# Products of attention weights and values in plain float32, two key blocks at a time in the halves of TensorE's columns

## The chip, the cores and the metric

The program runs on one core of one Trainium2 chip. The metric is the device time of one execution in microseconds (us); lower is better. The engines that matter are PE (TensorE, matmuls and transposes; PEld is its weight load), DVE (VectorE), ACT (ScalarE), POOL (GpSimd) and SP (SyncE, which issues DMAs).

## The reference, cut to what matters

One inference step of a two-layer encoder on 1024 prompt tokens and 8 x 16 sample tokens, width 1024, all in float32. The first layer's mixer runs 8 stick-breaking attention heads beside a convolution module; the second layer's mixer is banded softmax attention with 16 heads. Each layer ends in a squared-ReLU MLP. What the change touches is the last line of the first mixer's attention, the product of weights `w` and values `v` for the prompt tokens:

```python
def stick_breaking(q, k, v, q_pos, k_pos):
    z = jnp.einsum('bqhd,bkhd->bhqk', q, k).astype(jnp.float32) * (HEAD_DIM ** -0.5)
    mask = k_pos[None, :] < q_pos[:, None]
    log_keep = jnp.where(mask, jax.nn.log_sigmoid(-z), 0.0)
    between = lax.cumsum(log_keep, axis=3, reverse=True) - log_keep
    w = jnp.where(mask, jnp.exp(jax.nn.log_sigmoid(z) + between), 0.0)
    return jnp.einsum('bhqk,bkhd->bqhd', w.astype(v.dtype), v)
```

Heads have 64 channels. The mask is causal, so a block of 128 queries meets only the key blocks up to its own.

## The kernel before

**Split products.** Nearly all matmuls take operands in a rounded float32 type (`F32R`). To keep float32 accuracy, an operand is split into a high part (ACT copies it, rounding: L185) and a low part (DVE subtracts the high part from the source: L186), and high x high, high x low and low x high are summed. The helper `split` does both. A few products are in plain `F32` and need no split: the sample tokens' scores `zs` (L507, stationary operands 32 columns wide, four of them in the four quarters of the array's columns), the samples' products `so` (L541, likewise), the sums `mu` (L962), and the transposes.

**The first mixer** (`mixer0`) works through four pairs of heads, p = 0 to 3. Per pair there are 8 jobs (head i = 0, 1; query pair t = 0 to 3, that is 256 queries). A job computes scores `z` on PE (L865 to L868), sigmoids on ACT (L869, L870), a scan over `kp` (L848) and a product into `sg` (L850) on DVE, and then its weighing steps (`weigh_steps`): key blocks of 128 are gathered into groups of up to 512 columns, which here means two blocks a group; `turn` transposes a group's weights on PE into a PSUM bank `tpa` (L394) and splits it into `wha` (ACT) and `wla` (DVE); `prod` multiplies with the values. A job of query pair t has t + 1 groups, the last of which has 256 + 128 columns and the others 256 + 256, so there are 80 groups in all: 48 of 512 columns and 32 of 384. The stationary operand `vs` holds 128 columns per key block, the 64 high and the 64 low parts of the values, so one matmul gives the high sum in PSUM partitions 0 to 63 and the low one in 64 to 127; a group has four matmuls (`wha` and `wla` for each of two blocks, L406). `finish` copies the lower sum out (`ata`, L414, ACT) and adds the two halves (`cpa`, L416, DVE).

**Beside it** in the same stretch run the input projections of the next pair (`psp`, `psg`, `psa`, L225, PE, with their weights split into `hl_wi`), the sample tokens' attention, and the convolution: 124 taps, each one DVE instruction over 128 x 1024 and one over 128 x 128 (`y`, L674). `merge` interleaves the lists of steps by their declared PE time, with lags after a named step; `level` spreads the taps in proportion to the DVE time that the steps declare. The tile framework then schedules each engine's queue. Taps are traced inside `tc.issue_after(prior["weights"].ins)`: in DVE's queue a tap stands behind the instruction that `prior["weights"]` last named, which is the newest `wla`.

The second mixer uses the same `weigh_steps`.

Of the kernel before, what the change touches and what calls it, by code (L numbers as in the profile page):

```python
# [8 lines left out]
F32 = mybir.dt.float32  # L9
F32R = mybir.dt.float32r  # L10
AF = mybir.ActivationFunctionType
ALU = mybir.AluOpType
# [3 lines left out]
P = 128  # L16
# [7 lines left out]
HD = 64  # L24
# [13 lines left out]
PASS = 1 / 2.4  # L38


def f(ap):
    return ap.bitcast(F32)
# [56 lines left out]
def run(steps):  # L99
    for s in steps:  # L100
        s.go()
# [23 lines left out]
def tile_trunk(ctx, tc, ins, outs):  # L125
    nc = tc.nc
    ACT = nc.scalar.activation
    tt = nc.vector.tensor_tensor
    stt = nc.vector.scalar_tensor_tensor
    mm = nc.tensor.matmul  # L130
# [3 lines left out]
    def pool(name):  # L134
        return tc.tile_pool(name=name, bufs=1, reuse_waits="tile")
# [7 lines left out]
    def bank(name):  # L143
        return psum.tile([P, 512], F32, tag="ps", name=name)


    ident = const.tile([P, P], F32, name="ident")
# [35 lines left out]
    def split(hi, lo, src):  # L183

        ACT(hi, src, AF.Copy)  # L185
        return tt(lo, src, f(hi), ALU.subtract)  # L186

    prior = {}
# [184 lines left out]
    def weigh_steps(vs, wk, cat, i, t, blocks, name, scored):  # L373


        order = sorted(blocks.keys, key=lambda j: -len(blocks.keys[j]))
        groups, cur, used = [], [], 0
        for j in order:
            n = P * len(blocks.keys[j])
            if used + n > 512:  # L380
                groups.append((cur, used))
                cur, used = [], 0
            cur.append((j, used, n))
            used += n
        groups.append((cur, used))
        nmm = 2 * len(order)
        st = {"done": 0, "w": {}}

        def turn(gi):
            items, used = groups[gi]  # L390
            tp = bank(f"tp{name}{gi}")
            for j, c0, n in items:
                for q, tile_q in enumerate(blocks.keys[j]):
                    nc.tensor.transpose(tp[:, c0 + q * P:c0 + (q + 1) * P], blocks.get(j, tile_q), ident)  # L394
            wh = wk.tile([P, 512], F32R, tag="wt", name=f"wh{name}{gi}")
            wl = wk.tile([P, 512], F32R, tag="wt", name=f"wl{name}{gi}")
            prior["weights"] = split(wh[:, :used], wl[:, :used], tp[:, :used])
            st["w"][gi] = (wh, wl)

        def prod(gi):  # L400
            if gi == 0:
                st["av"] = bank(f"av{name}")
            for src in st["w"][gi]:
                for j, c0, n in groups[gi][0]:
                    o0 = 0 if 2 * t in blocks.keys[j] else P
                    mm(st["av"][:, o0:o0 + n], vs[:, j, i].rearrange("p a d -> p (a d)"), src[:, c0:c0 + n],  # L406
                       start=st["done"] == 0, stop=st["done"] == nmm - 1)
                    st["done"] += 1

        def finish():  # L410
            own = slice(64 * i, 64 * i + 64)
            av = st["av"]
            tmp = wk.tile([P, 256], F32, tag="av", name=f"at{name}")
            ACT(tmp[own], av[64:128, :256], AF.Copy)  # L414
            piece = wk.tile([P, 256], F32, tag="cat", name=f"cp{name}")
            tt(piece[own], av[0:64, :256], tmp[own], ALU.add)  # L416
            cat.put(piece, own, t * 256, 256)

        def pcost(gi):
            return sum(2 * max(n, 256) * PASS for _, _, n in groups[gi][0])  # L420

        def tcost(gi):
            return groups[gi][1] / P * 109

        last = len(groups) - 1
        def dcost(gi):
            return 60 + groups[gi][1] / 0.96

        def turns(gi):
            return Step(tcost(gi), lambda: turn(gi), dcost(gi), f"turn{name}{gi}", None if gi else scored, 4500)  # L430

        lag = 4500 if cat.layer == 0 else 2500

        def prods(gi):
            if gi < last:
                return Step(pcost(gi), lambda: prod(gi), 0.0, None, f"turn{name}{gi}", lag)
            return Step(pcost(gi), lambda: (prod(gi), finish()), 330.0, f"out{name}", f"turn{name}{gi}", lag)

        steps = [turns(0)]
        for gi in range(1, last + 1):  # L440
            steps += [turns(gi), prods(gi - 1)]
        steps.append(prods(last))
        return steps
# [150 lines left out]
    def mixer0():  # L594
        with ExitStack() as st:

            ep = Bufs(st.enter_context(pool("early0")), sg=3, kp=2)
            cp = Bufs(st.enter_context(pool("cache0")), ct=3)
# [5 lines left out]
            pp = Bufs(st.enter_context(pool("pair0")))  # L604
            wk = Bufs(st.enter_context(pool("work0")), wt=4, wts=1, cat=2)
# [3 lines left out]
            order = []  # L609
# [9 lines left out]
            at = {n: i for i, n in enumerate(order)}  # L619
            accs = []  # L620
            n0 = Next(0, rp, Lent(wk, "wt", 512), "h0", accs)
            h, rstd = n0.h, n0.r
# [209 lines left out]
            def expand_v(p, g):  # L832
                v = S["sv", p]
                tp = bank(f"vt0{p}{g}")
                for i in range(3):
                    c = (3 * g + i) * P
                    nc.tensor.transpose(tp[:, i * P:(i + 1) * P], v[:, c:c + P], ident)
                n = 3 if g < 2 else 2
                tv = tp[:, :n * P].rearrange("p (j h d) -> p j h d", j=n, h=2)
                dst = vs[:, 3 * g:3 * g + n]  # L840
                split(dst[:, :, :, 0, :], dst[:, :, :, 1, :], tv)
                if g == 2:
                    S["vn"] = pp.tile([P, P], F32, "vn", f"vn0{p}")
                    ACT(S["vn"], tp[:, 2 * P:3 * P], AF.Copy)
# [55 lines left out]

            start()
            qs, kd, kl = ([ep.tile([P, TP], F32R, f"{n}{i}", f"{n}{i}") for i in range(2)] for n in "qkl")
            vs = pp.tile([P, 8, 2, 2, HD], F32R, "vs", "vs0")
            run(level(proj(0), taps[:TAPS[0]]))
            taps = taps[TAPS[0]:]
            carry, cat_t = [], None
            for p in range(4):
                S["p"] = p
                expand_qk(p)
                if p < 3:  # L910
# [3 lines left out]
                    n = TAPS[p + 1]  # L914
# [8 lines left out]
                cat = Cat(0, p, wk, cat_t)  # L923
                jobs = attend(p, cat)
                body, left = pipeline(jobs[1:], jobs[0][2])
                steps = carry + [jobs[0][0]] + [Step(327.0, lambda p=p, g=g: expand_v(p, g)) for g in range(NG)]
# [111 lines left out]
    def mixer1(nx, win):  # L1038
        h, rstd = nx.h, nx.r
        with ExitStack() as st:  # L1040
            ep = Bufs(st.enter_context(pool("early1")), s=4, bp=2)
            cp = Bufs(st.enter_context(pool("cache1")), ct=2)
            pp = Bufs(st.enter_context(pool("pair1")))
            wk = Bufs(st.enter_context(pool("work1")), ss=1, wt=4, wts=2, cat=3, tot=4, mx0=4, mx1=4)
# [3 lines left out]
            vs = pp.tile([P, 8, 2, 2, HD], F32R, "vs", "vs1")  # L1048
# [79 lines left out]
            def attend(p, cat):  # L1128
                def job(i, t):
                    ws = {}  # L1130

                    def one(q):
                        n = min(q + 1, 5) * P
                        k0 = (q + 1) * P - n
                        b0 = 640 - n
                        s = ep.tile([P, 640], F32, "s", f"s{p}{i}{q}")
                        pieces = []
                        qc = slice(q * P, q * P + P)
                        for c, m in ((0, n),) if n <= 512 else ((0, 384), (384, 256)):
                            z = bank(f"zc{p}{i}{q}{c}")  # L1140
                            kc = slice(k0 + c, k0 + c + m)
                            mm(z[:, :m], qs[i][:, qc], kd[i][:, kc], start=True, stop=False)  # L1142
                            mm(z[:, :m], qs[i][:, qc], kl[i][:, kc], start=False, stop=True)  # L1143
                            pieces.append((z[:, :m], S["bp", p, i][:, b0 + c:b0 + c + m], c, m))
                        softmax(s, pieces, n, f"c{p}{i}{q}")
                        ws[q] = (s, k0)

                    q0, q1 = 2 * t, 2 * t + 1
                    keys = {j: [q for q in (q0, q1) if max(0, q - 4) <= j <= q] for j in range(max(0, q0 - 4), q1 + 1)}
                    blocks = Blocks(keys, lambda j, q: ws[q][0][:, j * P - ws[q][1]:j * P - ws[q][1] + P])  # L1150

                    def cost(q):
                        return 2 * max(256, min(q + 1, 5) * P) * PASS

                    name = f"c{p}{i}{t}"
                    return (Step(cost(q0), lambda: one(q0), 1100.0), Step(cost(q1), lambda: one(q1), 1100.0, f"z{name}"),
                            weigh_steps(vs, wk, cat, i, t, blocks, name, f"z{name}"))

                return [job(i, t) for i in range(2) for t in range(4)]

# [9 lines left out]
            for p in range(8):  # L1170
# [3 lines left out]
                cat = Cat(1, p, wk, cat_t)  # L1174
# [4 lines left out]
                steps = carry + [jobs[0][0]]  # L1179
                steps += [Step(327.0, lambda p=p, g=g: expand_v(p, g)) for g in range(NG)]  # L1180
                if p == 7:
# [3 lines left out]
                    steps = []  # L1185
# [524 lines left out]
    cat = mixer0()  # L1710
# [41 lines left out]
    cat = mixer1(n1, win)  # L1752
# [134 lines left out]
```

## Time and profile before

| | |
|---|---|
| median of 3 runs (lowest to highest) | 2791.39 us (2788.73 to 2793.07) |
| profiled execution | 2792.6 us |
| its span | 2790.7 us |
| PE, DVE, ACT, POOL busy | 96%, 77%, 50%, 12% |
| TensorE's mean granted clock | 0.988 of full speed |

The profiled execution's own time is its span and 1.9 us around it. Busy shares are means over the whole span; the first mixer lies in the first fifth of it, from about 99 us (the first pair's attention) to 586 us.

### The profile page before, as it was taken

The page shows a single profiled execution, that of the slowest core. Times are in us where ns is not written, and L with a number is a line of the kernel's source. Part 1 is how long each engine was busy: PE and PEld are TensorE (multiplying, and loading weights), DVE is VectorE, ACT ScalarE, POOL GpSimd, SP SyncE. Part 2 cuts the span into 40 slices and gives each one's busy share as a digit, 9 for nine tenths or more (in the row PEclk, how much of TensorE's full clock was granted, in tenths as well). Part 3 has the DMA queues.
Part 4 walks back from the last instruction along what each step waited for, and adds up shares of the span by engine and source line. Part 5 has one row for each costly group of instructions (what it writes and reads, how often), then busy time and mean ns, then how long its engine had stood idle before and what let it go on. Part 6 is the DMA issues. An engine that isn't in the chain of part 4 may idle for free.

```text
span 2790.7 us, 50667 instructions
## 1 busy us (share of the span) xinstructions
PE 2688.6 (96%) x19362; PEld 2582.7 (93%) x19362; DVE 2138.3 (77%) x4209; ACT 1389.7 (50%) x2898; POOL 329.3 (12%) x599
## 2 busy tenths in 40 slices
PE   8998988999999999999999999998999999999998
PEld 8987876789999999999999999997999999999998
DVE  8999999988777765758666777778787777647577
ACT  5344445755554453435355555555555555534344
POOL 1000101022111110000011111110231111100001
PEclk9999998999999999999999999999999999999999
DMA  4434346443343467534544444446543333684344
GB/s 155 128 96 127 121 128 194 155 166 131 139 144 144 147 236 250 152 94 146 160 142 137 138 138 138 138 133 211 186 137 139 139 139 135 223 273 137 96 125 142
DMA packets 173203, 422.90 MB, mean 152 GB/s; under 512 B 25968, under 2 KB 53808, under 8 KB 170912
## 3 DMA queue, kind: packets, MB, share of 16 engines
q1 hardware_dynamic: 135696, 288.38, 33.0%
q0 software_dynamic: 37120, 131.27, 13.7%
q8 instruction: 152, 2.49, 0.4%
q14 instruction: 91, 0.75, 0.1%
q10 hardware_dynamic: 144, 0.02, 0.0%
HBM read 289.60 MB, written 117.34 MB: 146 GB/s over the span
## 4 chain that ended last, share of the span: by engine, by line
PE 74%; DVE 17%; ACT 4%; issue 3%; DMA 2%; POOL 0%; DVEq 0%; SPq 0%; ACTq 0%; POOLq 0%
PE pd L1631 25%; PE um L1402 25%; PE psc L225 10%; DVE y L674 4%; DVE kp L848 3%; PE avc L406 2%; PE tpc L394 2%; PE psoa L225 1%; DVE sg L850 1%; PE f L225 1%; PE psob L225 1%; PE zc L1142 1%; DVE wla L186 1%; PE zc L1143 1%; PE psp L225 1%
## 5 line engine op out<-in xcount | busy, mean ns | idle before, releaser
L225 PE MATMUL psc<-h,hl_wc 128*128 128x384 f32 x1728 | 327.1, 339 | 0.0
L225 PEld LDWEIGHTS psc<-h,hl_wc 128*128 128x128 f32 x1728 | 296.8, 188 | 13.3 <-issue 10.9
L1402 PE MATMUL um<-sl,hl_m 128*128 128x288 f32 x1548 | 241.8, 297 | 0.0
L1402 PEld LDWEIGHTS um<-sl,hl_m 128*128 128x128 f32 x1548 | 219.0, 190 | 0.0
L1631 PE MATMUL pd<-tm,hl_wd 128*128 128x288 f32 x1584 | 214.7, 294 | 0.0
L1631 PEld LDWEIGHTS pd<-tm,hl_wd 128*128 128x128 f32 x1584 | 211.3, 189 | 0.0
L674 DVE SCALAR_TENSOR_TENSOR y<-u,dw,y 128x1024 f32<-128x1024 f32 (+1 forms) x232 | 176.4, 807 | 0.4
L225 PE MATMUL psp<-h,hl_wi 128*128 128x384 f32 x864 | 168.5, 344 | 0.2 <-ACT kps L897 0.2
L1409 ACT ACTIVATE hdm<-hdm 128x288 f32<-128x288 f32 x192 | 84.7, 442 | 156.5 <-DVE hdm L1408 154.8
L225 PEld LDWEIGHTS psp<-h,hl_wi 128*128 128x128 f32 x864 | 149.4, 190 | 6.4 <-issue 4.9
L186 DVE TENSOR_TENSOR tm<-xr,tm 128x576 fp32r<-128x576 f32 (+1 forms) x120 | 85.6, 714 | 90.7 <-ACT tm L185 87.0
L185 ACT ACTIVATE tm<-xr 128x576 fp32r<-128x576 f32 (+1 forms) x120 | 77.5, 646 | 92.1 <-PE pd L1631 74.0
L1402 PE MATMUL um<-sl,hl 128*128 128x288 f32 x756 | 119.1, 296 | 0.0
L1109 ACT ACTIVATE s<-s,mxc 128x640 f32<-128x640 f32 (+4 forms) x128 | 88.8, 694 | 59.6 <-DVE mxc L1106 57.9
L1631 PE MATMUL pd<-th,hl_wd 128*128 128x288 f32 x792 | 112.7, 295 | 3.4 <-DVE th L186 3.2
L1631 PE MATMUL pd<-xr,hl_wd 128*128 128x288 f32 x792 | 111.7, 294 | 0.0
L1631 PEld LDWEIGHTS pd<-th,hl_wd 128*128 128x128 f32 x792 | 107.3, 188 | 4.3 <-DVE th L186 3.7
L1631 PEld LDWEIGHTS pd<-xr,hl_wd 128*128 128x128 f32 x792 | 107.2, 189 | 0.0
L1402 PEld LDWEIGHTS um<-sl,hl 128*128 128x128 f32 x756 | 106.4, 188 | 0.8
L1631 PE MATMUL pd<-tm,hl 128*128 128x288 f32 x768 | 104.9, 295 | 0.0
L1631 PEld LDWEIGHTS pd<-tm,hl 128*128 128x128 f32 x768 | 103.1, 188 | 0.0
L1106 DVE CUSTOM_DVE_ANT_0 s<-zc,bp 128x384 f32<-128x384 f32 (+3 forms) x128 | 66.0, 516 | 39.1 <-PE zc L1143 37.1
(527 smaller groups left out, 6774.3 us busy)
## 6 DMA issues: line engine op xcount, KB each, us to landing
xr<-hb_d SPq DMA_DIRECT2D x208, 288.0 KB, 3.0
xr<-in_w_up_dram SPq DMA_DIRECT2D x64, 512.0 KB, 4.2
hb_d<-hdm POOLq DMA_DIRECT2D x96, 288.0 KB, 2.4
hb_d<-t POOLq DMA_DIRECT2D x96, 288.0 KB, 2.4
wm<-in_w_down_dram SPq DMA_DIRECT2D x64, 256.0 KB, 4.2
st_wd<-in_w_down_dram SPq DMA_DIRECT2D x64, 256.0 KB, 3.7
st_wc<-in_w_in_c_dram SPq DMA_DIRECT2D x44, 256.0 KB, 2.9
xm_d<-xo POOLq DMA_DIRECT2D x16, 576.0 KB, 3.6
```

The source lines that it names most:

```text
L185: ACT(hi, src, AF.Copy)
L186: return tt(lo, src, f(hi), ALU.subtract)
L225: mm(ps()[:, :G], hl[:, a, at:at + P], act[g][k // 4][b][:, k % 4, :], start=n == 0, stop=n == len(todo) - 1)
L394: nc.tensor.transpose(tp[:, c0 + q * P:c0 + (q + 1) * P], blocks.get(j, tile_q), ident)
L406: mm(st["av"][:, o0:o0 + n], vs[:, j, i].rearrange("p a d -> p (a d)"), src[:, c0:c0 + n], start=st["done"] == 0, stop=st["done"] == nmm - 1)
L674: stt(src if j == CW - 1 else dst, src, wj, dst, ALU.mult, ALU.add)
L848: nc.vector.tensor_tensor_scan(keep[:, 0:n][:, ::-1], keep[:, 0:n][:, ::-1], ones[:, 0:1].to_broadcast([P, n]), 1.0, ALU.mult, ALU.mult)
L1106: nc.vector.tensor_tensor_reduce(s[:, c:c + m], z, b, -1.0, mx, ALU.add, ALU.min, new)
L1109: ACT(s[:, :n], s[:, :n], AF.Exp, bias=mx, scale=-1.0, accum_out=tot)
L1402: mm(banks[b, n][:, :TQ], w[:, a, c * P:c * P + P], combo(key, c)[:, h, n * TQ:n * TQ + TQ], start=k < 3 and c == 0 and i == 0, stop=c == ...
L1409: ACT(y, y, AF.Relu)
L1631: mm(ps, w[:, a, m * P:m * P + P], b[:, h, (n - ns[0]) * TQ:(n - ns[0]) * TQ + TQ], start=first and s == 0, stop=j == NJ - 1 and s == 2, s ...
```

## The change

The first mixer gets a new `weigh_steps`; the second keeps the old one under the name `split_weigh_steps`. In the new one a group's transposed weights are copied once, in plain float32, by ACT (`wa`, no `wla`); the values are kept in plain float32 (`vs` is half as large, one ACT copy and no subtraction); and a group of two key blocks is two matmuls with 64 stationary columns each, the first block's into PSUM partitions 0 to 63 and the second's into 64 to 127. `finish` adds the two halves as before, and for t = 0, where the second block reaches only 128 of the 256 queries, copies the other 128 from the first half alone. The groups have the same blocks and the declared PE times come out the same; the turns no longer declare DVE time; the tag `wt` with its 4 buffers now holds one tile a group, not two; and `prior["weights"]` now names the newest `cpa`, once a job.

```diff
         order = sorted(blocks.keys, key=lambda j: -len(blocks.keys[j]))
+        groups = []
+        for two in zip(order[::2], order[1::2]):
+            n, m = (P * len(blocks.keys[j]) for j in two)
+            groups.append(([(two[0], 0, n), (two[1], n, m)], n + m))
+        st = {"w": {}}
+
+        def turn(gi):
+            items, used = groups[gi]
+            tp = bank(f"tp{name}{gi}")
+            for j, c0, n in items:
+                for q, tile_q in enumerate(blocks.keys[j]):
+                    nc.tensor.transpose(tp[:, c0 + q * P:c0 + (q + 1) * P], blocks.get(j, tile_q), ident)
+            st["w"][gi] = wk.tile([P, 512], F32, tag="wt", name=f"w{name}{gi}")
+            ACT(st["w"][gi][:, :used], tp[:, :used], AF.Copy)
+
+        def prod(gi):
+
+            if gi == 0:
+                st["av"] = bank(f"av{name}")
+            for m, (j, c0, n) in enumerate(groups[gi][0]):
+                o0 = 0 if 2 * t in blocks.keys[j] else P
+                mm(st["av"][64 * m:64 * m + 64, o0:o0 + n], vs[:, j, i], st["w"][gi][:, c0:c0 + n], start=gi == 0,
+                   stop=gi == last)
+
+        def finish():
+            own = slice(64 * i, 64 * i + 64)
+            av = st["av"]
+            one = P if t == 0 else 0
+            tmp = wk.tile([P, 256], F32, tag="av", name=f"at{name}")
+            ACT(tmp[own, one:], av[64:128, one:256], AF.Copy)
+            piece = wk.tile([P, 256], F32, tag="cat", name=f"cp{name}")
+            if one:
+                ACT(piece[own, :one], av[0:64, :one], AF.Copy)
+            prior["weights"] = tt(piece[own, one:], av[0:64, one:256], tmp[own, one:], ALU.add)
+            cat.put(piece, own, t * 256, 256)
+
+        def pcost(gi):
+            return 4 * groups[gi][0][0][2] * PASS
...
+        def turns(gi):
+            return Step(tcost(gi), lambda: turn(gi), 0.0, f"turn{name}{gi}", None if gi else scored, 4500)
...
+    def split_weigh_steps(vs, wk, cat, i, t, blocks, name, scored):
...
-            prior["weights"] = split(wh[:, :used], wl[:, :used], tp[:, :used])
+            split(wh[:, :used], wl[:, :used], tp[:, :used])
...
-                tv = tp[:, :n * P].rearrange("p (j h d) -> p j h d", j=n, h=2)
-                dst = vs[:, 3 * g:3 * g + n]
-                split(dst[:, :, :, 0, :], dst[:, :, :, 1, :], tv)
+                ACT(vs[:, 3 * g:3 * g + n], tp[:, :n * P].rearrange("p (j h d) -> p j h d", j=n, h=2), AF.Copy)
...
-            vs = pp.tile([P, 8, 2, 2, HD], F32R, "vs", "vs0")
+            vs = pp.tile([P, 8, 2, HD], F32, "vs", "vs0")
...
-                            weigh_steps(vs, wk, cat, i, t, blocks, name, f"z{name}"))
+                            split_weigh_steps(vs, wk, cat, i, t, blocks, name, f"z{name}"))
```

The order of PE's queue is nearly kept. This is PE near the end of pair 0 (last job but one group; `psp` is the next pair's projection, `tpa` the transposes, `ava` the products), before:

```order
L225 MATMUL psp_2241<-h_30_171,hl_wi_0_1816 128x384
L394 MATMUL tpa_2254<-ident,sg_1957 128x128
L394 MATMUL tpa_2254<-ident,sg_2017 128x128 x2
L406 MATMUL ava_2218<-wha_2163,vs_747 128x256 x2
L406 MATMUL ava_2218<-wla_2164,vs_747 128x256 x2
L225 MATMUL psp_2241<-h_40_178,hl_wi_1_1821 128x384
L225 MATMUL psp_2241<-h_41_179,hl_wi_1_1821 128x384
```

and of the change:

```order
L225 MATMUL psp_2182<-h_30_171,hl_wi_0_1776 128x384
L388 MATMUL tpa_2195<-ident,sg_1912 128x128
L388 MATMUL tpa_2195<-ident,sg_1970 128x128 x2
L398 MATMUL ava_2161<-wa_2108,vs_747 64x256 x2
L225 MATMUL psp_2182<-h_40_178,hl_wi_1_1781 128x384
L225 MATMUL psp_2182<-h_41_179,hl_wi_1_1781 128x384
```

The group stands at the same place, behind the next group's transposes and between two halves of a projection's matmuls; its four matmuls of 128 rows are two of 64 (64x256 is the shape written).

This is DVE at the end of pair 0 (the last scan `kp` and its `sg`, the job's closing add `cpa`, and `l`, `q`, which belong to the next pair's expansion), before:

```order
L848 SCALAR_TENSOR_TENSOR kp_2226<-kp_2226,ones 128x1024
L816 TENSOR_TENSOR sv_2156<-psp_2167,rh_315 128x384
L850 TENSOR_TENSOR sg_2225<-sg_2225,kp_2226 128x1023
L186 TENSOR_TENSOR wla_2259<-tpa_2254,wha_2258 128x384
L674 SCALAR_TENSOR_TENSOR u_389<-u_389,dw,y_1236 128x1024
L674 SCALAR_TENSOR_TENSOR u_389<-u_389,dw,y_1236 128x8x16
L577 COPY cs_1918<-sq_2282 64x64 x2
L416 TENSOR_TENSOR cpa_2295<-ava_2218,ata_2293 64x256
L351 TENSOR_TENSOR l_745<-sk_1914,k_743 64x1024
L351 TENSOR_TENSOR l_746<-sk_1914,k_744 64x1024
L353 SCALAR_TENSOR_TENSOR q_742<-sq_1181,q_742 64x1024
```

and of the change:

```order
L879 TENSOR_TENSOR sv_2101<-psp_2110,rh_315 128x384
L737 SCALAR_TENSOR_TENSOR u_389<-u_389,dw,y_1239 128x1024
L737 SCALAR_TENSOR_TENSOR u_389<-u_389,dw,y_1239 128x8x16
L351 TENSOR_TENSOR l_745<-sk_1870,k_743 64x1024
L351 TENSOR_TENSOR l_746<-sk_1870,k_744 64x1024
L353 SCALAR_TENSOR_TENSOR q_742<-sq_1178,q_742 64x1024
L909 SCALAR_TENSOR_TENSOR kp_2167<-kp_2167,ones 128x1024
L640 COPY cs_1874<-sq_2219 64x64
L911 TENSOR_TENSOR sg_2166<-sg_2166,kp_2167 128x1023
L640 COPY cs_1874<-sq_2219 64x64
L410 TENSOR_TENSOR cpa_2230<-ava_2161,ata_2228 64x256
```

The subtraction `wla` is gone, the expansion's `l`, `l`, `q` stand now ahead of the last scan instead of behind the closing add, and `cpa` stands behind all of them; the next taps `y` (of the new convolution channel block) follow `cpa`.

## Rows read from the trace of the kernel before

**Rows 1.** The page: busy us by engine, and the span in 40 slices of 70 us.

```profile
PE 2688.6 (96%) x19362; PEld 2582.7 (93%) x19362; DVE 2138.3 (77%) x4209; ACT 1389.7 (50%) x2898; POOL 329.3 (12%) x599
...
PE   8998988999999999999999999998999999999998
...
DVE  8999999988777765758666777778787777647577
...
PEclk9999998999999999999999999999999999999999
```

**Rows 2.** Busy time by engine in four stretches of the first mixer.

```profile
core 0: us, PE busy (x) PEld busy (x) DVE busy (x) ACT busy (x) POOL busy (x), PEclk, DMA share, GB/s
99.00:227.00 128.00, 117.92 (x846) 106.27 (x844) 124.67 (x172) 55.66 (x126) 10.17 (x19) 0.99 0.38 118
227.00:352.00 125.00, 111.60 (x801) 97.34 (x797) 124.60 (x176) 56.38 (x127) 12.06 (x21) 1.00 0.43 123
352.00:445.00 93.00, 79.33 (x603) 67.44 (x601) 92.61 (x127) 44.84 (x106) 11.77 (x21) 0.94 0.46 139
445.00:586.00 141.00, 122.35 (x799) 99.76 (x800) 126.87 (x230) 96.40 (x209) 11.32 (x21) 0.92 0.50 164
```

**Rows 3.** Chain that ended last within 227:352 us, its shares by line.

```profile
by line: DVE y L674 31.3%; DVE kp L848 16.3%; issue 15.2%; DVE sg L850 8.1%; DVE wla L186 7.9%; DVE hl_wi L186 4.0%; DVE cpa L416 2.5%; DVE kps L848 2.0%; DVE l L351 2.0%; DVE y L671 1.6%; DVE u L674 1.2%; DVE sgs L850 1.1%; DVE vs L186 1.0
```

**Rows 4.** Who PE waited for in 99:586 us: total us, times, longest us.

```profile
PE ava L406 <- DVE wla L186: 15.1, 18, 2.5
PE tpa L394 <- DVE sg L850: 8.5, 11, 1.9
...
PE z L865 <- DVE cpa L416: 3.8, 3, 2.2
PE z L865 <- DVE wla L186: 2.5, 1, 2.5
```

**Rows 5.** The same stretches, instructions that touch wla alone.

```profile
99.00:227.00 128.00, 6.82 (x32) 4.90 (x32) 9.83 (x16) 0.99 0.38 118
227.00:352.00 125.00, 8.70 (x40) 6.21 (x40) 12.35 (x20) 1.00 0.43 123
352.00:445.00 93.00, 7.26 (x32) 5.26 (x32) 10.46 (x17) 0.94 0.46 139
445.00:586.00 141.00, 12.62 (x56) 9.30 (x56) 16.56 (x28) 0.92 0.50 164
```

**Rows 6.** The same for vs, the sum of the stretches (PE, PEld, DVE, ACT).

```profile
sum 487.00, PE 61.18 PEld 48.41 DVE 5.67 ACT 5.03; mean PE 15.30 PEld 12.10 DVE 1.42 ACT 1.26
```

**Rows 7.** Groups of instructions in 0:900 us: the closing add and its copy (busy, mean ns, idle before).

```profile
L416 DVE TENSOR_TENSOR cpa<-ava,ata 64x256 f32<-64x256 f32 x32 | 13.2, 414 | 0.6
...
L414 ACT ACTIVATE ata<-ava 64x256 f32<-64x256 f32 x32 | 12.2, 380 | 39.6 <-PE ava L406 39.2
```

**Rows 8.** PE in order of time (start us, us, ..., count), around one product group.

```profile
299.88 0.23 PE L868 MATMUL z<-maskd,unit 128*128 128x128 f32 x1
299.95 0.45 PE L406 MATMUL ava<-wha,vs 128*128 128x256 f32 x2
300.23 0.40 PE L406 MATMUL ava<-wla,vs 128*128 128x256 f32 x2
300.47 2.24 PE L225 MATMUL psp<-h,hl_wi 128*128 128x384 f32 x12
302.55 0.49 PE L394 MATMUL tpa<-ident,sg 128*128 128x128 f32 x3
```

**Rows 9.** PE in order of time, around products in quarters of the columns.

```profile
106.94 0.93 PE L837 MATMUL vt<-ident,sv 128*128 128x128 f32 x7
107.80 0.64 PE L507 MATMUL zs<-ct00k,qb 128*32 128x256 f32 x8
108.37 1.34 PE L225 MATMUL psp<-h,hl_wi 128*128 128x384 f32 x6
```

**Rows 10.** PE in order of time, plain float32 products over all columns.

```profile
462.70 2.85 PE L962 MATMUL mu<-yl,ones 128*128 128x384 f32 x8
```

More of the change, by code (lines that the diff above doesn't have):

```diff
@@ new lines, in pcost, with tcost, prods @@
+        def pcost(gi):
+            return 4 * groups[gi][0][0][2] * PASS
+        def tcost(gi):
+            return groups[gi][1] / P * 109
+        last = len(groups) - 1
+        def turns(gi):
+            return Step(tcost(gi), lambda: turn(gi), 0.0, f"turn{name}{gi}", None if gi else scored, 4500)
+        lag = 4500 if cat.layer == 0 else 2500
+        def prods(gi):
+            if gi < last:
+                return Step(pcost(gi), lambda: prod(gi), 0.0, None, f"turn{name}{gi}", lag)
+            return Step(pcost(gi), lambda: (prod(gi), finish()), 330.0, f"out{name}", f"turn{name}{gi}", lag)
@@ L377, in weigh_steps @@
+        steps = [turns(0)]
+        for gi in range(1, last + 1):
+            steps += [turns(gi), prods(gi - 1)]
+        steps.append(prods(last))
+        return steps
+    def split_weigh_steps(vs, wk, cat, i, t, blocks, name, scored):
+        order = sorted(blocks.keys, key=lambda j: -len(blocks.keys[j]))
         groups, cur, used = [], [], 0
```

## The prediction

> **What bounds the kernel now.** I read the page first: PE is busy 96% of the span, but its row of slices has 8s and a 7 only at the start, up to about 590 us, and there DVE stands at 9 nearly throughout, while from slice 10 on PE is full and DVE is not [rows 1]. The change touches only this first part. So I cut it at the expansions of the four head pairs, into 128, 125, 93 and 141 us, and asked for busy times [rows 2]: DVE is busy 124.7, 124.6, 92.6 and 126.9 us of them, that is 97.4, 99.7, 99.6 and 90%; PE 117.9, 111.6, 79.3 and 122.4, that is 92, 89, 85 and 87%. ACT is busy 43 to 48%, in the last stretch 68%. The chain within the second stretch consists of DVE work almost alone, the taps first (31%), then the scans, with `wla` at 8% [rows 3]. The waits of PE say the same from the other side: it waits above all for DVE, 15.1 us for `wla` before the products, 8.5 for `sg` before transposes, 3.8 for `cpa`, 2.5 for `wla` before a score [rows 4]. In three of the four stretches, then, DVE sets the length and PE has 10.1, 13.4 and 13.7 us to spare; in the fourth neither is full (PE has 18.7 to spare). That is 55.9 us of PE's time in all.
>
> **What is removed.** All `wla` subtractions: 9.8, 12.4, 10.5 and 16.6 us of DVE by stretch, 49.2 in all [rows 5]. The subtractions on `vs`, 5.7 us [rows 6], 1.4 a stretch. Together 54.9 us, after which DVE has 113.4, 110.9, 80.8 and 108.9 us of work. ACT's side stays: it made `wha` and the high part of `vs` with the same shapes as it now makes `wa` and `vs`; for t = 0 one copy of 256 columns becomes two of 128, and its price of 0.38 us for the whole [rows 7] at most doubles, 8 x 0.4 = 3 us on an engine half idle. I cost that at nothing: the work that hides it is PE's own, and without that cover it would be these 3 us.
>
> **What is added on PE.** Before, a product group is four matmuls. Between 300.23 and 300.47 two of 256 columns take 0.24 us, 0.12 each; a rounded matmul of 128 columns takes 0.07 (299.88 to 299.95) [rows 8]. So a group of 512 columns costs 0.48 us and one of 384 costs 0.38. After, a group is two plain float32 products in halves of the array. The trace has no halves; its nearest rows are the sample scores, plain float32, 256 columns, in quarters [rows 9]. There four products show as eight records (each product passes twice) and the next matmul starts 0.57 us after the first. Getting in costs something: the seven transposes ahead are 0.11 apart (from 0.93 us for seven and 0.49 for three [rows 8, 9]), so their turn is over at 107.71, and `zs` starts at 107.80, 0.09 later. Getting out does too: a projection matmul takes (302.55 - 300.47) / 12 = 0.173 us in a stream and 0.34 by itself (2.24 less 11 x 0.173), so six of them should show as 1.21 us, and behind `zs` they show as 1.34, 0.13 more. Sum: 0.57 + 0.09 + 0.13 = 0.79 us for a group. Lower bound: two passes with no cost of entry or exit. A pass of 384 plain columns takes some 0.33 us (eight in 2.85, with the tail of the last [rows 10]), one of 256 thus 0.22 and two 0.44. Upper bound: the halves do not overlap, four passes, 0.88 + 0.35 = 1.23. I take 0.79, since two halves are two of these quarters joined. Then PE gains 48 x (0.79 - 0.48) + 32 x (0.79 - 0.38) = 28.0 us, 0.35 a group. With 16, 20, 16 and 28 groups in the stretches (half of the PE records on `wla` [rows 5]) that is 5.6, 7.0, 5.6 and 9.8 us, and PE's work becomes 123.5, 118.6, 84.9 and 132.2 us, 459.2 in all.
>
> What speaks against the change is this exit and entry. The Trainium skill says so too: by "TensorEngine Tiling (Array Packing)", Tiling Modes, changing the tiling mode drains TensorE. The trace agrees, with 0.09 us before and 0.13 behind `zs` beyond what its passes take. With the figure of "TensorE: Matmul & The Clock Gate", Step-by-step, a drain of about 128 cycles, two drains would be an estimated 0.11 us, a group 0.55, and PE would gain only 9 us; the measured rows decide for 28.
>
> **What the waits do.** The products no longer wait for DVE: `wa` comes from ACT, and the 15.1 us at `ava` and 2.5 at `z` (a PSUM bank that `wla` held) go. What is late next is `sg`, and PE's transposes behind it. One wait is added: taps now queue behind the newest `cpa`, which needs the job's last product and then `ata`. DVE idles only 0.6 us before all 32 `cpa` now [rows 7], and the order shows `cpa` placed behind other work still. If DVE met each one early, it could lose two passes of 0.22 and `ata`'s 0.38, some 0.9 us with what lies between, 32 x 0.9 = 29 us, and behind it stand taps and the next job's scans, for which PE's transposes wait. DVE's spare time after the change (below, some 60 us) covers that on average, so I put it at nothing. The moved `l`, `l`, `q` ahead of the last scan can cost PE a few us once a pair if the carried job comes late.
>
> **The sum.** Both engines now need nearly the same time, PE a little more: PE becomes the bound. It will not be full. DVE as the bound reached 97.4 to 99.7%; I give PE 97% in three stretches, since its queue is in order and still needs DVE's scans, and 96% in the last: 127.3 + 122.3 + 87.5 + 137.7 = 474.8 against 487, 12.2 us less. One more term: the granted clock is 0.94 and 0.92 in the last two stretches [rows 2], at the lower of its levels after PE had idled, which is 0.06 x 93 + 0.08 x 141 = 17 us of PE's time. With fewer waits I let a quarter of that come back, 4 us. So 16 us off 2792.6, or 2776.6; the median of the runs shown is 1.2 lower than the profiled execution, and I say **2776 us**.
>
> **The rivals.**
> *A, PE is packed to the brim.* If the taps fill DVE's holes as well as they do now and every wait of PE goes, the stretches shrink to 459.2 us, 28 less, 2765, and with half of the clock's 17 us back 2757. For it: DVE did reach 99.7%. Against: two engines at 93% or more that wait for each other.
> *B, slower: the halves do not overlap.* Then a group costs 1.23 us, PE gains 48 x 0.75 + 32 x 0.85 = 63 us against 56 to spare, and with up to 19 us of its other waits left (half of the 38 that are not for `wla`) the time is 7 to 26 us longer, 2800 to 2819. It decides from 56 / 80 = 0.70 us more per group, 1.14 us a group. For it: nothing in rows of halves, since there are none. Against: eight records of quarters in 0.64 us [rows 9], where eight passes in a row would take 1.8.
> In a sentence apart: "TensorE: Matmul & The Clock Gate", Part 3, The mechanism, calls matmuls strict FIFO in start and end, by which the second pass of the first half would hold up the second half (three passes in a row; with 0.22 us for entry and exit an estimated 0.88 us a group, 35 us more on PE instead of 28, and 2783 us); the quarters do not show that.
> *C, no change.* DVE's time is freed, but the waits move to `sg` and `cpa`: of PE's idle 55.9 us the 17.6 at `wla` go, and of the other 38 only some 5 to 15, not the 23 that the forecast takes. With 28 us of new work that is 431 + 28 + (23 to 33) = 482 to 492 us for the stretches, 2788 to 2798; if none of the 38 goes, 2803. For it: a scan is as long as before, and what waits for `sg` waits for its chain, not for a free DVE. Against: in the first three stretches no engine but DVE was late in most of the waits [rows 4].
>
> **Chances.** The forecast, 2764 to 2786 us, 0.58; A, 2757 to 2764, 0.12; C within 2786 to 2797, 0.16, and beyond, 0.04; B 0.10. A measurement of this kernel can tell about 0.2%, 5.6 us. So faster 0.70, same 0.16, slower 0.14. The range takes in A and most of C, 2757 to 2795, and leaves out B and what lies below A.
>
> **What would show it.** Right: a group's two products with starts a few ns apart and the next matmul 0.5 to 0.6 us later; DVE busy at 93% or less in the first three stretches with PE at 96% or more; no wait of `ava` for DVE; the stretches 10 to 25 us shorter together, and nothing changed behind 600 us. Wrong: two products of a group 0.4 us or more apart (B); PE's waits for `sg` and DVE's before `cpa` grown by 10 us or more (C); a group that costs under 0.6 us (A).

## The result, and the profile after

The changed kernel took 2761.27 us (median of 4 runs, 2760.88 to 2763.31) against 2790.06 us before (4 runs, 2788.17 to 2793.07): ratio 0.9897, 95% interval 0.988 to 0.9914. That is 28.8 us or 1.03% less; 16 us less was forecast. The direction was right, the size was not: it came out at nearly twice the forecast. The time lies outside the forecast's own interval (2764 to 2786) and inside that of rival A (2757 to 2764); the wide range (2757 to 2795) held it only because it took in A.

The page of the changed kernel, its busy times and slices of 69 us, answers to [rows 1]:

```profile
PE 2681.8 (97%) x19362; PEld 2556.6 (93%) x19362; DVE 2093.9 (76%) x4117; ACT 1388.9 (50%) x2906; POOL 329.4 (12%) x599
...
PE   8999998999999999999999999998999999999998
...
DVE  8999997888777755758577777778787777647577
...
PEclk9999998999999999999999999999999999999999
```

Two of PE's first slices rise from 8 to 9 (the fourth and the sixth), and DVE's row loses its 9s in slices 7 and 8. The first matmul of the first MLP (`um`) starts at 612.8 us, where it started at 643.2; from there to the end it is 2146.9 us against 2147.5. So the gain, 30.4 us in the profiled executions, lies ahead of the MLP, in the first mixer. (In the runs below that leave the part behind it alone, that part takes 2142.6 to 2148.7 us, so profiled stretches are good to a few us.)

To compare like with like I cut both traces at the transposes of each pair's values (`vt`) and at the last product, since the change moved the pairs' expansions, at which the prediction had cut. The busy times of the kernel before, the last row from 99 us to the first `um`:

```profile
core 0: us, PE busy (x) PEld busy (x) DVE busy (x) ACT busy (x) POOL busy (x), PEclk, DMA share, GB/s
106.70:239.10 132.40, 122.32 (x888) 108.70 (x885) 129.04 (x179) 56.98 (x127) 12.20 (x22) 0.99 0.45 132
239.10:362.00 122.90, 109.34 (x790) 94.52 (x789) 122.44 (x173) 56.75 (x129) 11.13 (x19) 1.00 0.40 120
362.00:474.30 112.30, 94.35 (x654) 78.20 (x653) 107.48 (x151) 57.65 (x133) 12.27 (x22) 0.89 0.48 147
474.30:583.70 109.40, 95.57 (x664) 80.10 (x664) 99.96 (x189) 77.95 (x169) 8.66 (x16) 0.95 0.47 158
99.00:643.20 544.20, 488.39 (x3372) 427.89 (x3371) 514.22 (x769) 285.14 (x625) 70.60 (x106) 0.97 0.46 142
```

and of the changed kernel (same columns):

```profile
106.50:234.30 127.80, 121.72 (x886) 100.69 (x884) 125.54 (x169) 57.45 (x130) 12.24 (x22) 1.00 0.49 145
234.30:350.80 116.50, 110.09 (x797) 91.58 (x797) 112.30 (x151) 56.35 (x133) 11.25 (x19) 0.99 0.41 126
350.80:448.30 97.50, 86.72 (x648) 66.53 (x647) 85.62 (x113) 56.71 (x134) 12.20 (x22) 0.95 0.51 159
448.30:552.60 104.30, 95.74 (x658) 73.70 (x658) 88.83 (x163) 76.92 (x170) 8.63 (x16) 0.95 0.50 166
99.00:612.80 513.80, 481.97 (x3371) 399.66 (x3370) 468.74 (x677) 283.74 (x632) 69.66 (x105) 0.98 0.48 150
```

The stretches shrank by 4.6, 6.4, 14.8 and 5.1 us. Over the whole, DVE's busy time fell by 45.5 us (514.2 to 468.7). PE's fell too, by 6.4 (488.4 to 482.0), where the prediction had it rise by 28. DVE is now at 98, 96, 88 and 85% of the stretches and PE at 95, 94, 89 and 92%: neither is full in all of them. The prediction's sign of being right, DVE at 93% or less in the first three with PE at 96% or more, did not come.

PE's waits in 99:555 us (total, times, longest), which answer to [rows 4]:

```profile
PE tpa L388 <- DVE sg L911: 19.3, 11, 3.3
PE psa L225 <- DVE u L717: 2.7, 2, 1.6
PE ava L398 <- ACT wa L390: 2.5, 3, 1.9
PE z L926 <- DVE cpa L410: 2.4, 1, 2.4
```

No product waits for DVE any more. What is late now is `sg`, 19.3 us against 8.5, in front of the transposes.

Two groups on PE. The changed kernel, in order of time:

```profile
141.72 0.69 PE L225 MATMUL psg<-h,hl_wi 128*128 128x384 f32 x3
142.34 0.65 PE L398 MATMUL ava<-wa,vs 128*64 128x256 f32 x4
142.92 0.33 PE L584 MATMUL sn<-ident,sgs 128*128 128x128 f32 x1
143.09 0.27 PE L590 MATMUL st<-ident,sgs 128*128 128x128 f32 x1
```

The four passes of a group (two products, two passes each) begin at 142.34 and the next matmul at 142.92, 0.58 us later: the halves overlap. Taken one by one, the records start in two pairs, 7 ns apart within a pair. Finally the busy time of all instructions on `ava` (PE, PEld, DVE, ACT), from 99 us to the first `um`, in the changed kernel, where [rows 6] gave 61.18 us of PE before:

```profile
99.00:612.80 513.80, 51.28 (x320) 17.15 (x320) 12.23 (x32) 13.49 (x40) 0.98 0.48 150
```

### The profile page after: what moved, and what is told of

It is laid out like the page before. It is cut to its first block, busy times and chain, and to the rows that moved or that the text cites. A ratio compares the mean times of both kernels' runs of the same rounds, so it can differ in the third digit from the quotient of the medians.

```text
span 2759.7 us, 50582 instructions
## 1 busy us (share of the span) xinstructions
PE 2681.8 (97%) x19362; PEld 2556.6 (93%) x19362; DVE 2093.9 (76%) x4117; ACT 1388.9 (50%) x2906; POOL 329.4 (12%) x599
## 4 chain that ended last, share of the span: by engine, by line
PE 82%; DVE 10%; ACT 3%; DMA 2%; issue 2%; SPq 0%; DVEq 0%; ACTq 0%; POOLq 0%
PE pd L1692 25%; PE um L1463 25%; PE psc L225 10%; PE psp L225 5%; PE avc L469 2%; PE psoa L225 2%; PE tpc L457 2%; DVE y L737 1%; DVE kp L909 1%; PE f L225 1%; PE zs L570 1%; PE zc L1203 1%; PE psob L225 1%; PE zc L1204 1%; PE ava L398 1%
## 5 line engine op out<-in xcount | busy, mean ns | idle before, releaser
L225 PEld LDWEIGHTS psc<-h,hl_wc 128*128 128x128 f32 x1728 | 296.8, 188 | 13.3 <-issue 10.9
L185 ACT ACTIVATE whc<-tpc 128x512 fp32r<-128x512 f32 (+1 forms) x144 | 72.4, 523 | 46.5 <-PE tpc L457 45.6
```

The lines of the kernel that those rows point to most:

```text
L225: mm(ps()[:, :G], hl[:, a, at:at + P], act[g][k // 4][b][:, k % 4, :], start=n == 0, stop=n == len(todo) - 1)
```

## Experiments

Each is compared with the kernel before on its own chip; "the ratio of the change" is 0.9897, and 0.001 of a ratio is 2.8 us; the 95% intervals are some 0.0015 either way, 4 us. The stretch is 99 us to the first `um`: 544.2 us before, 513.8 in the change.

**The change again.**

> The changed kernel once more, beside the next two on one chip: 2758 to 2765, ratio 0.988 to 0.991.

2761.99 us, 0.9897 (0.9879 to 0.9915): the ratio holds when it is measured again.

**Old products, no low part.** Based on the kernel before:

```diff
+            if cat.layer == 0:
+                ACT(wh[:, :used], tp[:, :used], AF.Copy)
+                st["w"][gi] = (wh, wh)
+                return
...
-            prior["weights"] = split(wh[:, :used], wl[:, :used], tp[:, :used])
+            split(wh[:, :used], wl[:, :used], tp[:, :used])
...
+            if cat.layer == 0:
+                prior["weights"] = add
```

The turns of the first mixer also declare no DVE time, as in the change.

> The kernel before, with the weights' low part left out in the first mixer: the products take the high part twice (wha, wha), so PE has its old four full-width matmuls a group, DVE has no wla, and taps queue behind cpa as in the change. The low part is left out of the result. If PE sets the length of the first mixer after the change (the forecast's view, groups of 0.79 us against 0.44), this is some 15 to 25 us faster than the changed kernel: 2736 to 2746. If DVE's work and the chain through its scans set it, PE's cheaper groups bring little: 2755 to 2768 (5.7 us of subtractions on vs are back).

2763.12 us, 0.9891 (0.9876 to 0.9906), as fast as the change. Its stretch (columns as above: length, PE, PEld, DVE, ACT, POOL, clock):

```profile
99.00:616.80 517.80, 474.37 (x3370) 428.46 (x3369) 474.06 (x689) 283.36 (x625) 71.06 (x106) 0.96 0.47 150
```

and its instructions on `ava`:

```profile
99.00:616.80 517.80, 52.73 (x320) 45.75 (x320) 13.21 (x32) 12.17 (x32) 0.96 0.47 150
```

This run shows two things. PE's old full-width groups, with no wait for DVE, do not make the kernel faster than the halves do, so PE's price of a group did not by itself set the length after the change. (DVE has 5.3 us more to do here, the subtractions on `vs`, which may hide a few us.) And PE shows 474.4 us where the kernel before, with the same matmuls, shows 488.4: 14 us of what the profile counted there as busy went away with the subtraction and its wait, with no change in PE's work and at no higher clock (0.96, before 0.97). The old groups by themselves show 52.7 us in place of 61.2.

The same group as above, in this run:

```profile
141.15 0.86 PE L225 MATMUL psg<-h,hl_wi 128*128 128x384 f32 x4
141.84 0.64 PE L410 MATMUL ava<-wha,vs 128*128 128x256 f32 x4
142.32 0.28 PE L527 MATMUL sn<-ident,sgs 128*128 128x128 f32 x1
142.43 0.60 PE L533 MATMUL st<-ident,sgs 128*128 128x128 f32 x4
```

From its start to the next matmul it takes 0.48 us, as the prediction had it, against 0.58 in the change. With a projection matmul at 0.173, the group starts 0.17 us behind the start of the last projection, in the change 0.27; and `st` follows `sn` by 0.11, in the change by 0.17. So by starts the halves cost 0.10 + 0.10 + 0.06, some 0.25 us more here. Compared so in both timelines, groups with full-width matmuls on both sides mostly cost 0.25 to 0.31 us more; two groups in a row share one entry and exit, and beside the samples' products in quarters the difference is at most 0.12. The mean over the 73 groups that can be compared so is 0.20 us, which makes 16 us for all 80, an estimate.

**Dead subtraction.** The change, plus:

```diff
+            idle = wk.tile([P, 512], F32, tag="wt", name=f"wd{name}{gi}")
+            tt(idle[:, :used], tp[:, :used], st["w"][gi][:, :used], ALU.subtract)
```

and the turn's declared DVE time as before.

> The changed kernel, with the old subtraction put back on DVE as dead work: it reads the transposed weights and wa and writes a tile that nothing reads, so DVE has its 49 us again and the PSUM bank is held as long, but no product waits for it. If the change paid by DVE's work, nearly all of the gain goes: 2785 to 2800. If it paid by the wait of the products for wla, the gain stays: 2761 to 2770. In between, the two share it.

2784.64 us, 0.9968 (0.9956 to 0.998). Of the change's 29 us some 20 are gone, with no product waiting for the subtraction. The stretch:

```profile
99.00:637.40 538.40, 494.42 (x3378) 403.06 (x3377) 508.86 (x758) 285.51 (x633) 70.16 (x105) 0.97 0.46 144
```

40.1 us more of DVE's busy time lengthen it by 24.6, 0.61 to the microsecond (0.5 by the ratios). DVE's work is what most of the gain was made of; the time fell just short of the range set for it (2785 to 2800). A rest of some 9 us is left. Some 3 of it are DVE's too, since the 5.4 us of subtractions on `vs` were not put back (508.9 us, before 514.2). Two more things show here. PE's busy time is 494.4 us, 12.4 above the change with the same matmuls and with no product waiting for DVE; the clock (0.97, in the change 0.98) makes some 5 of them. So it is not the products' wait alone that stretches PE's busy time. And the dead subtraction holds the PSUM bank of the transposes as `wla` did: PE waits 5.6 us for it in all, so up to that much of the loss is the bank's and not DVE's load; no run separates the two.

**Fewer buffers.** `wt=4` becomes `wt=2` in the change, the depth that the dead subtraction leaves.

> The changed kernel with 2 buffers for the transposed weights instead of 4, so that two groups are in flight as in the kernel before and in the dead subtraction's kernel. If that depth was part of what the dead subtraction took away, 2766 to 2775; if it was DVE's work alone, 2759 to 2765.

2762.22 us, 0.9898 (0.9881 to 0.9916): the depth took no part.

**The wait alone.** The change, plus one column copied by DVE:

```diff
+            nc.vector.tensor_copy(st["w"][gi][:, 0:1], tp[:, 0:1])
```

> The changed kernel with a DVE copy of one column into each wa: the products wait for DVE again as they did for wla, the PSUM bank is held until DVE has read it, and DVE's work grows by 80 small instructions, 5 to 15 us. With the change paid by DVE's work and not by this wait: 2763 to 2771, the small instructions' share. If the wait was worth the 9 us that the dead subtraction left, 2770 to 2780.

2770.6 us, 0.9918 (0.9901 to 0.9935), on the border of the two expectations; its interval touches that of the change. PE's waits in 99:570 us:

```profile
PE ava L399 <- DVE wa L391: 18.4, 11, 3.7
PE tpa L388 <- DVE sg L912: 4.2, 6, 1.8
```

The wait of the products is back in full (18.4 us, before 15.1), but `sg` is waited for 4.2 us and not 19.3: PE, held up at one place, is no longer held up at the other. Its stretch:

```profile
99.00:624.40 525.40, 490.05 (x3382) 404.25 (x3381) 475.56 (x759) 284.08 (x632) 69.67 (x106) 0.97 0.47 148
```

The 6.8 us of DVE work that the copies add are worth some 4 us at the dead subtraction's rate of 0.61 (24.6 / 40.1). The whole loss is 6 us by the ratios and 9 by the medians, which leaves 2 to 5 us for the wait by itself, an estimate within the noise.

**One half.** The change with both blocks in the same half of the columns:

```diff
-                mm(st["av"][64 * m:64 * m + 64, o0:o0 + n], ...
+                mm(st["av"][0:64, 256 * m + o0:256 * m + o0 + n], ...
...
-            ACT(tmp[own, one:], av[64:128, one:256], AF.Copy)
+            ACT(tmp[own, one:], av[0:64, 256 + one:512], AF.Copy)
```

> The changed kernel with both key blocks' products in the same half of the columns, so that they cannot overlap (the second block's sums go to other columns of the same PSUM bank): four passes in a row, some 0.44 us more a group, 35 us more PE work over 80 groups. If PE sets the length after the change, the time goes up by 25 to 35 us: 2786 to 2796. If DVE does, PE's 32 us of idle time in the stretch take most of it: 2763 to 2780.

2774.47 us, 0.9931 (0.9914 to 0.9948), 9 to 13 us slower than the change, within the second range. The same group in its timeline, and its stretch:

```profile
143.19 1.08 PE L398 MATMUL ava<-wa,vs 128*64 128x256 f32 x4
144.20 0.33 PE L584 MATMUL sn<-ident,sgs 128*128 128x128 f32 x1
```

```profile
99.00:626.10 527.10, 504.85 (x3372) 419.26 (x3371) 469.92 (x677) 282.88 (x633) 70.65 (x105) 0.98 0.46 147
```

1.01 us from the group's start to the next matmul, in place of 0.58: this is the price of halves that do not overlap. It puts 22.9 us on PE's busy time, of which 13.3 reach the length. PE's work does count after the change, then, at about 0.6 to the microsecond (0.4 by the ratios). Even so the kernel stays faster than before.

**Both mixers.** The second mixer calls the new `weigh_steps` too, with `vs` in float32.

> The change in the second mixer as well, where PE is busy 97% and DVE 74%. There the price of a group on PE should show nearly bare: 144 groups at 0.79 us against the 0.55 us (79 us / 144) that PE spends from one product to the next in the trace, +35 us, less 2 to 9 us of waits that go: 2787 to 2797. If the entry and exit of the halves cost nothing that matters, 2755 to 2765, since DVE and PE both have less to do.

2771.98 us, 0.9924 (0.9907 to 0.9941): some 7 to 11 us slower than the change, less than a third of the 35 expected, and between the two ranges. PE's busy time in the second mixer, from shortly before its attention until after it, in the change and in this kernel (the windows are 1339 to 1990 and 1341 to 2001):

```profile
1339.00:1990.00 651.00, 632.41 (x4488) 597.87 (x4488) 476.30 (x1296) 346.00 (x793) 84.45 (x183) 0.99 0.49 151
```

```profile
1341.00:2001.00 660.00, 652.78 (x4489) 556.00 (x4488) 394.31 (x1127) 346.67 (x808) 83.24 (x182) 0.99 0.48 148
```

DVE loses 82 us of work and the mixer still gets longer; PE is busy 652.8 of 660 us, so here PE sets the length. For 144 groups PE shows 20.4 us more, 0.14 us a group, where the prediction's difference of price was 0.35; 11.4 of them go into PE's idle time (18.6 to 7.2 us) and 9.0 into the length. By starts, as above, the groups cost 0.19 us more on the mean.

**Where taps may stand.** In the change, taps stand behind the newest `cpa`; this order is called the guard here. The first run leaves it out (first edit), the second puts it on `sg` (both edits):

```diff
-            prior["weights"] = tt(piece[own, one:], av[0:64, one:256], tmp[own, one:], ALU.add)
+            tt(piece[own, one:], av[0:64, one:256], tmp[own, one:], ALU.add)
```

```diff
-                tt(w[:, 0:n - 1], w[:, 0:n - 1], keep[:, 1:n], ALU.mult)
+                prior["weights"] = tt(w[:, 0:n - 1], w[:, 0:n - 1], keep[:, 1:n], ALU.mult)
```

> The changed kernel without the order that keeps taps behind the newest cpa. If waiting behind cpa cost DVE little (as the trace of the change says: 3.4 us of DVE idle in front of cpa), nothing moves much: 2758 to 2768. If the guard cost DVE holes, it gets faster, down to 2750; if it kept taps out of the way of the scans, slower, 2768 to 2780.

2769.1 us, 0.992 (0.9905 to 0.9935): slower by 6 to 8 us, just above the range for "nothing moves" and in that for a guard that keeps taps out of the way of the scans. The intervals of the two overlap, so it is shown that the guard costs nothing, and only likely that it is worth something.

> The changed kernel with taps kept behind the newest sg instead of the newest cpa, since PE's largest wait after the change is now tpa for sg (19 us). If DVE's scans are late because taps stand in front of them, PE gets some of the 19 us back: 2748 to 2758. If they are late because DVE has no room, nothing changes: 2758 to 2768.

2765.04 us, 0.99 (0.9885 to 0.9915): the same as the change. PE's wait for `sg` fell only from 19.3 to 16.5 us. So holding taps behind `sg` does not cure the wait: the order of taps is not the main reason why `sg` is late.

**Lighter taps.** The change, with the taps' second instruction only in the first and the last tap of a channel block:

```diff
-                    for dst, src in pairs:
+                    for dst, src in pairs[:2 if j in (0, CW - 1) else 1]:
```

> The changed kernel without the taps' small instruction (the sample tokens' 128 columns) in 29 of 31 taps: that part of the convolution is left out. It takes some 24 us of DVE work out of the first mixer's attention, of another kind than the change did. If DVE's work still sets the length there, 8 to 16 us come off: 2745 to 2753. If PE sets it after the change, at most 4: 2757 to 2762.

2750.39 us, 0.9851 (0.9836 to 0.9865), some 11 to 13 us faster than the change. The stretch:

```profile
99.00:606.60 507.60, 481.85 (x3373) 399.59 (x3372) 451.26 (x588) 283.68 (x632) 69.91 (x105) 0.98 0.49 154
```

17.5 us less DVE work, 6.2 us less length there (the profiled executions differ by 3 us more behind the mixer, where nothing was changed). DVE still counts after the change, at about 0.35 to the microsecond by the stretch and 0.6 to 0.7 by the medians and ratios.

**Taps on POOL.** The same instruction done by POOL, nothing left out:

```diff
...
+                            m = cv.tile([P, P], F32, "m", f"m{c}{j}").rearrange("p (b t) -> p b t", t=16)
+                            nc.gpsimd.tensor_scalar(m, src, wj, None, ALU.mult)
+                            nc.gpsimd.tensor_tensor(src if j == CW - 1 else dst, m, dst, ALU.add)
```

> The changed kernel with the taps' small instruction (the sample tokens' 128 columns) done on POOL, as a product into a scratch tile and an add, and nothing left out. DVE loses the same 24 us in the attention as when they were left out; POOL gets 240 instructions more. If POOL keeps up and does not slow DVE, 8 to 13 us come off as they did there: 2748 to 2754. If DVE's other instructions get slower beside POOL, or the tap chain now waits for POOL at the end of a channel block, 2760 or more.

2833.21 us, 1.0153 (1.0135 to 1.017): 72 us slower than the change. POOL's new instructions (count, busy us, mean ns, idle before) and one of DVE's waits:

```profile
L741 POOL TENSOR_SCALAR m<-u,dw 128x128 f32<-128x128 f32 x120 | 127.5, 1063 | 25.5 <-DMA u<-in_conv_in_dram 14.2
L742 POOL TENSOR_TENSOR y<-m,y 128x128 f32<-128x128 f32 x116 | 102.8, 887 | 21.3 <-DVE y L734 12.1
```

```profile
DVE cpa L410 <- DMA cat_d<-cpa: 35.9, 2, 20.8
```

Two instructions of 1.06 and 0.89 us on POOL take the place of one of 0.34 on DVE, and POOL's queue is also the one that issues the stores of `cpa` and the copies of the expansion. They come late, buffers stay taken, and DVE waits 35.9 us in two waits for a store of `cpa`. That is half of the loss; the rest was not followed.

## Why the prediction came out as it did

**What bounds the kernel: right.** In the first mixer DVE set the length, and taking work off DVE shortened it. The dead subtraction shows it from the other side. After the change the chain that ended last has PE's projection first (18.0% of the stretch), then DVE's taps (8.0%) and scans (7.7%), where the taps led before with 19.3% and the scans with 13.6%. So PE did come onto the path, but not alone.

**What is removed: right, a little less.** 54.9 us were counted from busy times of the instructions removed; DVE's busy time fell by 45.5. Its instructions overlap at their ends in the records, and the busy time counts that overlap once: the dead subtraction's own instructions add up to 49.3 us and raise DVE's busy time by 40.1, the same share.

**What is added on PE: the step that failed.** "Then PE gains 28.0 us", and "PE's work becomes ... 459.2 us in all". The same part of the change, from 99 us to 2.3 us behind the last product, reads (columns as in [rows 2]):

```profile
99.00:554.90 455.90, 424.07 (x3039) 341.95 (x3038) 421.42 (x607) 251.63 (x574) 45.38 (x81) 0.97 0.47 146
```

PE is busy 424.1 us, where it was 431.2: a loss of 7.1 instead of a gain of 28.0. Two things were wrong with the term.

The smaller one is the price. By starts the old group was priced well (0.48 us), and the new one too for a group that stands alone between full-width matmuls (0.25 to 0.31 us more, forecast 0.31 to 0.41). But entry and exit were charged to each of the 80 groups, and many share them with a neighbour: some 16 us and not 28.

The larger one is the base. The 28 us were added to a busy time, and that busy time was not PE's work alone: it shrank when DVE's load and the waits went. The run with old products has the old matmuls and 14 us less. [Rows 6] had a sign of it: 61.18 us for 80 groups, 0.76 us each, where 0.48 and 0.38 were taken for the old price; without the wait they show 52.7. A record of PE that is followed by idle time counts in full, 0.30 us on the mean in the kernel before, and one in a stream only until the next start, 0.12 to 0.17 [rows 8]; counted in the timelines, PE falls idle 78 times in the stretch before, 36 times with the old products alone and 23 times in the change, which makes some 9 us as an estimate. The rise of the clock makes some 6 (below). The rest of the 23 us (16 + 7) was not followed. The Trainium skill, "Perfetto Trace Analysis", Identifying the Most-Contended Engine, says that TensorE's matmul busy share is not a good measure of how close a kernel is to its limit, since pipelined instructions look smaller in the trace. The conclusion holds here, but the deviation goes the other way: some 14 of 488 us were more than the matmuls needed.

**The waits: right in kind.** Those at `wla` went, and `sg` is late next, as said. It grew by 11 us, which the prediction had named as a sign of rival C. In this C was right: PE idles 31.8 us of the part above (455.9 less 424.1), within C's 23 to 33, where the forecast's sum left 15.6. C failed by the other half of its sum, PE's 28 us of new work. The guard behind `cpa` costs nothing, as costed: DVE's idle time in front of `cpa` in the change is 1.9 and 2.1 us (the number behind the second bar, with what ended it):

```profile
L410 DVE TENSOR_TENSOR cpa<-ava,ata 64x256 f32<-64x256 f32 x24 | 10.0, 416 | 1.9 <-ACT ata L406 1.4
L410 DVE TENSOR_TENSOR cpa<-ava,ata 64x128 f32<-64x128 f32 x8 | 2.2, 281 | 2.1 <-ACT cpa L409 1.6 <-PE z L927 0.4
```

**The sum: two errors of opposite sign.** PE at 97% of 459.2 us gave 474.8 us for four stretches. Measured are 424.1 us at 93%, that is 455.9 us: PE's busy time was forecast 35.1 us too high and its idle time 16.2 too low. That the two partly cancel was luck; with PE's busy time right and 97% kept, the sum would have been 437 us, as far off on the other side. What counts after the change is neither engine alone: a microsecond of work put on DVE costs 0.5 to 0.6, one put on PE 0.4 to 0.6 (one half), one more taken off DVE gives 0.35 to 0.7. At 0.5 to 0.6, the 45.5 us that DVE lost make 23 to 28 us. The clock's share was forecast at 4 us; the mean granted clock went from 0.97 to 0.98 over the stretch, which is 0.03 x 544.2 - 0.02 x 513.8 = 6 us of PE's time.

**The rivals.** A had the time, 2757 to 2764, but not the mechanism: PE is not packed, it idles some 32 us of the stretch (513.8 less 482.0). B is excluded by the trace, and its price was tested: a group that takes 1.01 us, and with the 0.09 and 0.13 of the prediction 1.23, leaves the kernel still faster than before, so the point from which B was to decide, 1.14 us a group, was set too low by the same error.

The Trainium skill, "TensorE: Matmul & The Clock Gate", Part 3, The mechanism, calls matmuls strict first-in first-out in start and end. The prediction worked out from it a second half held up behind the first half's second pass; the trace does not show that for these halves, whose four passes take 0.58 us where the same four in one half take 1.01.

**What stays open.** How the 29 us split between DVE's work and the wait is known only roughly: some 20 by the dead subtraction, up to 5.6 of them perhaps the PSUM bank's, some 3 for the work on `vs`, and 2 to 5 for the wait by the copied column. Why the third stretch gained most (14.8 us) was not tested; its granted clock rose from 0.89 to 0.95, which is 0.11 x 112.3 - 0.05 x 97.5, some 7 us of PE's time. None of the variants that kept the whole computation beat the change.

## What to carry to other kernels

When an edit replaces a group of instructions on an engine that waits a lot, do not add a price taken from starts to a busy time taken from the trace: part of that busy time is stretched by the waits and goes when they go. Price the old and the new group by the same measure, with the neighbours that they really have, and ask separately what the busy time would be without the waits; a run with the old group and no wait tells. Where two engines stand at 90% or more and feed each other, neither bound alone gives the answer; a dose of dead work on either one measures what a microsecond of it is worth.

## What the runs showed of the hardware that was not expected

Two plain float32 products in the two halves of the columns take 0.58 us to the next matmul, where the same two in one half take 1.01. Entry and exit come on top, as later starts of the group (0.10 us) and of the matmul behind the next one (0.06 in the rows shown). Against four full-width rounded matmuls that makes 0.25 to 0.31 us more between full-width neighbours, and 0.20 on the mean. And small elementwise instructions are dear on POOL: 1.06 and 0.89 us for 128 x 128 elements, for 0.34 us of DVE's fused one (the profile's spans on POOL are rough).
